# A hybrid mLSTM and differential-attention block: gate chain two pairs later, one branch gate ahead of the first q and k, merged mLSTM loads

## The chip, the cores and the metric

The kernel runs on one core of one Trainium2 chip, in one launch. The metric is the device time of that launch in microseconds (us). A core has five engines that run beside each other, each with its own instruction queue taken strictly in order: PE (TensorE, matrix products and transposes), DVE (VectorE), ACT (ScalarE), POOL (GpSimd) and SP (SyncE, which issues most of the DMAs). An instruction that has to wait holds up everything behind it on its own engine.

## The reference, cut to what matters

One layer on x of 1 x 1024 x 1024 in fp32. A normalised input is projected onto twelve segments; an mLSTM with four heads of 256 runs in both directions over one group of them, a differential attention with eight heads over another, and two gates mix the branches:

```python
h = rmsnorm(x, norm_g)
a_q, a_k, a_v, a_o, a_z, a_g, b_q, b_k, b_v, b_z, g_a, g_b = split(h @ w_in)
qk = silu(centred_depthwise_conv(concat(a_q, a_k), ml_conv_w))      # width 5
i, log_f = gates from a_g + ml_gate_b                               # 4 x 4 heads, both directions
y_a = mlstm(q, k, v, i, log_f) forward + reversed, normed, gated by a_o and a_z
y_b = (softmax(q1 k1) - lam * softmax(q2 k2)) v per head, rope, normed, gated by b_z
mix = sigmoid(g_a) * (y_a @ w_branch_a) + sigmoid(g_b) * (y_b @ w_branch_b)
out = rmsnorm(x + mix @ w_out, final_g)
```

(The last lines are told in short; the change touches none of them.)

## The kernel before, in words

**Arithmetic.** Every fp32 product is made of two float32r parts, a high one (H) and a low one (L), so a product is three matmuls: high by high, low by high, high by low. The splitting into H and L is done by ACT, DVE and POOL.

**Stages, in the order of PE's instructions.** (1) The opening: load x, normalise, transpose, first products. (2) Eighteen "pairs" of projections, numbered 0 to 17 from the list `self.pairs`: pairs 0 and 1 are wide v pairs (`wide_units`, L394, with the sink `v_sink`, L427), the others alternate a k or q pair with an o and z pair (`pair_units`, L349; sinks `conv_sink` and `oz_sink`). Each pair's products go to PSUM banks tagged T, six of them, and a sink (adds, convolution, gating on DVE, ACT and POOL) must empty a bank before PE writes it again. The products of pair i are woven with the last products of pair i - 1; a stretch of this loop is called slot i here. The sinks store the convolved q and k in DRAM tiles `cd` and v in `vd`. (3) The first head's q and k (`qk[0]`), its gate z, and the first part of v for attention (`v0`, L573). (4) Eight attention heads, each a row of eight cycles. A cycle of PE has a group of scores (S, L1062: two tiles of 128 x 1024 in PSUM, which DVE reduces, L1065, and ACT exponentiates, L1067, before PE may write them again), transposes (T) of earlier probabilities e, of att and of rb_y (L132), and the products with v. Between these, `w.weave` spreads filler: projections for the next heads and, in the last head, branch gates. (5) The mLSTM (`ml_units`), which loads k, q, v and the gates' rows back from DRAM (`load_k` L1179, `load_parts` L1185, `load_gb` L1190, `load_v` L1198, all on SP) and has nine branch gates as filler. (6) The two branch products, the mix and the output.

**Branch gates.** `gate_units` makes one gate: 48 matmuls of 128x512 in two halves. Each half ends with a tanh on ACT (`gt`, L959, one buffer) and a store into DRAM (`tgb` or `tga`, L960). During the opening and the mLSTM the store is issued by ACT, elsewhere by SP. `fill(n)` takes the next n gates of the list `gq`; `FILL[h]` says how many go into head h.

**mLSTM gates.** `ml_gates` gives pieces: the loading of the gates' weights and their products (`gl`, `gmm`), `rows` (a row computation of logs, exponentials and scans on DVE and ACT, L842 to L879, in tiles `gch`), `chain`, `weights` and `columns`. `angle_loads` gives pieces of the rotary tables (angles, then sine and cosine, which the first q and k are multiplied by at L984 to L995). The dictionary `more` puts each piece ahead of a given unit of a given pair.

**What sets the order.** PE runs in the order in which the units are added (`keep(E.PE)`). The order on DVE, ACT, POOL and SP is made by a scheduler at build time, which may move an instruction far from its place in the code; at run time each engine follows that order.

Of the kernel before, what the change touches and what calls it, by code (L numbers as in the profile page):

```python
# [36 lines left out]
INF = 1.0e9  # L37
FILL = (0, 0, 0, 0, 0, 0, 0, 2)
Z_EARLY = (0, 1, 3, 5)
# [71 lines left out]
class Block:  # L111
# [353 lines left out]
    def conv_sink(self, seg, n):  # L465
# [3 lines left out]
        def sink(i, j, ps, rest):  # L469
# [16 lines left out]
            for half in range(2):  # L486
                o = half * 512


                at = lambda x: self.cd[x][2 * n + i][:, o:o + 512]  # L490
                acc = self.psA.tile([128, 512], F32, name="pj", tag="pj", bufs=2)
                th = self.s0.tile([128, 512], F32, name="tz", tag="tz", bufs=2)
                a.mul(acc, raw[:, o:o + 512], w(0))  # L493
                for x in range(1, 5):
                    v.scalar_tensor_tensor(out=acc, in0=raw[:, o + x:o + x + 512], scalar=w(x), in1=acc, op0=ALU.mult, op1=ALU.add)  # L495
                a.activation(out=th, in_=acc, func=AF.Tanh, scale=0.5)
                yh, H = y[:, o:o + 512], raw[:, o:o + 512]
                v.scalar_tensor_tensor(out=yh, in0=th, scalar=1.0, in1=acc, op0=ALU.add, op1=ALU.mult)
                if seg == "ak":
                    self.q.dma_start(out=at("ak"), in_=yh)  # L500
                a.copy(H.bitcast(F32R), yh)
                self.q.dma_start(out=at(seg + "H"), in_=H)
                lo = th if seg == "ak" else yh
                p.tensor_tensor(out=lo.bitcast(F32R), in0=yh, in1=H, op=ALU.subtract)
                self.q.dma_start(out=at(seg + "L"), in_=lo)
        return sink
# [446 lines left out]
    def gate_units(self, seg, i):  # L953
        key = ("w_in", OFF[seg] + 128 * i)
        idx = (0 if seg == "ga" else 8) + i

        def done(half, ps):
            t = self.wpool.tile([128, 512], F32, name="gt", tag="gt")
            self.a.activation(out=t, in_=ps, func=AF.Tanh, scale=0.5, bias=self.gbh[:, idx:idx + 1])  # L959
            (self.a if self.opening or self.ml else self.q).dma_start(out=self.tg[seg][i][:, half * 512:(half + 1) * 512], in_=t)  # L960
        return sum((self.proj(key, half, lambda ps, half=half: done(half, ps)) for half in range(2)), [])
# [205 lines left out]
    def ml_head(self, n, st):  # L1167
# [8 lines left out]
        def load_k(c):  # L1176
            x = loc["ak", c] = w2.tile([128, 2, L], F32, name="akf", tag=f"kf{c}", bufs=1)
            for i in range(2):
                q.dma_start(out=x[:, i], in_=self.cd["ak"][2 * n + i][:, c * L:(c + 1) * L])  # L1179

        def load_parts(seg, c):
            st[seg, c] = tuple(w2.tile([128, 2, L], F32R, name=seg + y, tag=f"{seg}{y}{c}", bufs=1) for y in "HL")
            for x, y in zip(st[seg, c], "HL"):
                for i in range(2):
                    q.dma_start(out=x[:, i].bitcast(F32), in_=self.cd[seg + y][2 * n + i][:, c * L:(c + 1) * L])  # L1185

        def load_gb(c):
            for d in range(2):
                t = loc["gb", d, c] = w2.tile([128, L], F32, name="gb", tag=f"gb{d}{c}", bufs=1)
                q.dma_start(out=t, in_=self.gg[d, row(c):row(c) + 1, :].broadcast_to([128, L]))  # L1190

# [64 lines left out]
        def scores(tt):  # L1256
# [11 lines left out]
            for d in range(2):  # L1268
# [3 lines left out]

                p.affine_select(out=W[:, lo:hi], in_=loc["gb", d, c][:, lo:hi], pattern=[[-sg, hi - lo]], compare_op=ALU.is_ge,  # L1273
                                fill=-1.0e30, base=sg * (b * 128 - lo), channel_multiplier=sg)
# [101 lines left out]
    def ml_units(self, heads, gates):  # L1376
# [6 lines left out]
        hl = lambda x, c: x["gb"](c) + x["HL"](c)  # L1383
        for c in (3, 2, 1):
            un += x["k"](c) + x["v"](c)
        un += take(8) + x["weigh"](3, 1) + take(3) + x["state"](3, 1) + hl(x, 0)
        un += x["weigh"](2, 1) + take(5) + x["state"](2, 1) + x["k"](0) + x["v"](0)
        un += x["weigh"](1, 1) + take(4) + x["state"](1, 1) + x["split"](0) + hl(x, 1)
        un += take(4) + x["S"](0)
# [176 lines left out]
    def build(self):  # L1566
# [21 lines left out]
        with pool(name="const", bufs=1) as self.const, \  # L1588
# [18 lines left out]
            self.ya, self.yb, self.gd_ml = dt("ya"), dt("yb"), dt("gm")  # L1607
            self.cd = {n: dt("c" + n) for n in ("ak", "akH", "akL", "aqH", "aqL")}
            self.vd = {x: [[self.dram.tile([128, 512], F32, name=f"av{x}{n}_{c}") for c in range(NC)] for n in range(NH_A)] for x in "HL"}
# [60 lines left out]
            ang = [do(lambda: next(gen)) for _ in range(19)]  # L1670
            more = {(1, 0): gl + gmm}
            for (i, k), step, un in (((2, 6), 1, rows[:6]), ((4, 6), 2, rows[6:]), ((6, 6), 2, chain), ((6, 13), 1, ang[:1]),
# [3 lines left out]
                for j, u in enumerate(un):  # L1676
                    more.setdefault((i + (k + step * j) // 14, (k + step * j) % 14), []).append(u)

# [10 lines left out]
            qk, z = zip(*[self.da_proj(h, sts[h]) for h in range(NH_B)])  # L1689
            w.add(do(lambda: setattr(self, "ahead", True)), *qk[0], *z[0])  # L1690
            v0 = self.da_v(0, sts[0:2])
            w.add(*v0[:20])
            prev = None
# [92 lines left out]
```

## Time and profile before

| | before |
|---|---|
| median of 3 runs | 1704.09 us (1699.93 to 1706.28) |
| the profiled execution | 1703.18 us |
| its span in the profile | 1701.1 us |
| mean granted TensorE clock | 0.993 |
| busy: PE / DVE / ACT / POOL | 97% / 60% / 46% / 39% |
| DMA engines over the span | 117 GB/s; 191.05 MB of 199.76 MB on the queue of SP and ACT |

The span is the time from the first to the last instruction on the profile's record; the execution's own time has 2.1 us more around it. An instruction row has its start (us), its duration (us), engine, line, operation and tiles, and in brackets how long its engine had been idle and what ended the wait. Matmuls are pipelined: a matmul's own duration is longer than the distance from its start to the next one's, and it is the distance that counts for time.

### The profile page before, as it was taken

Reading aid. Unit: us, or ns where it says so; the run is one execution under the profiler, and the core shown is the slowest. Engines: PE = TensorE matmul, PEld = TensorE weight load, DVE = VectorE, ACT = ScalarE, POOL = GpSimd, SP = SyncE. Lnnn points to the kernel's source line nnn. Section 1 sums busy time; section 2 is a strip of 40 time slices with the busy share of each in tenths; the row PEclk is TensorE's granted clock in tenths of the full one; section 3 lists DMA queues with packets and bytes.
Section 4 is the critical chain, followed back from the end, with each engine's and each line's share of the span. In section 5 each row is a group of like instructions: output and inputs, shape, how many; then the busy total and the mean of one; then the engine's idle time right before and its main releaser. Section 6 shows DMA issues by size and latency. Waiting matters only on the chain. (4 is left out here: it accounts for less than half of the span.)

```text
span 1701.1 us, 25404 instructions
## 1 busy us (share of the span) xinstructions
PE 1644.1 (97%) x9335; PEld 1379.2 (81%) x9335; DVE 1025.1 (60%) x1817; ACT 775.9 (46%) x1548; POOL 660.0 (39%) x713
## 2 busy tenths in 40 slices
PE   7989999999999999999999999999999998999998
PEld 5879877778888788878878887888888876888887
DVE  5654677776754776777677677604566664235533
ACT  6433455555533455455554545524566554122221
POOL 5744666666653451524345152132132221222000
PEclk9999999999999999999999999999999999999999
DMA  5433344343342223213131221238866527453222
GB/s 183 133 109 119 125 145 149 116 137 118 130 142 69 73 54 86 69 35 85 38 100 40 73 70 44 62 102 255 257 212 204 156 75 269 145 172 101 75 91 83
DMA packets 191246, 199.76 MB, mean 117 GB/s; under 512 B 13465, under 2 KB 144882, under 8 KB 191122
## 3 DMA queue, kind: packets, MB, share of 16 engines
q1 hardware_dynamic: 187186, 191.05, 37.2%
q10 hardware_dynamic: 3936, 7.09, 1.1%
q8 instruction: 73, 1.20, 0.3%
q14 instruction: 51, 0.42, 0.1%
HBM read 124.60 MB, written 56.72 MB: 107 GB/s over the span
## 5 line engine op out<-in xcount | busy, mean ns | idle before, releaser
L551 PE MATMUL pj<-hH,wH 128*128 128x512 f32 x640 | 268.4, 419 | 1.9 <-ACT f L664 1.5
L551 PE MATMUL pj<-hH,wL 128*128 128x512 f32 x640 | 252.4, 394 | 1.6 <-POOL wL L210 1.6
L551 PE MATMUL pj<-hL,wH 128*128 128x512 f32 x640 | 251.3, 393 | 0.2 <-DVE hL L702 0.2
L1067 ACT ACTIVATE e<-S,nm 128x1024 f32<-128x1024 f32 x128 | 142.5, 1114 | 96.6 <-DVE nm L1065 96.3
L212 POOL TENSOR_TENSOR wL<-raw,wH 128x1024 fp32r<-128x1024 f32 x34 | 83.7, 2462 | 216.6 <-ACT wH L207 212.9
L1065 DVE TENSOR_REDUCE nm<-S 128x1 f32<-128x1024 f32 x128 | 150.6, 1218 | 21.7 <-PE S L1062 21.1
L551 PEld LDWEIGHTS pj<-hH,wH 128*128 128x128 f32 x640 | 121.4, 190 | 33.4 <-issue 13.1
L551 PEld LDWEIGHTS pj<-hH,wL 128*128 128x128 f32 x640 | 120.6, 188 | 31.0 <-POOL wL L210 3.6
L551 PEld LDWEIGHTS pj<-hL,wH 128*128 128x128 f32 x640 | 121.4, 190 | 17.6 <-DVE hL L702 0.6
L1087 DVE TENSOR_TENSOR pL<-T,pH 128x512 fp32r<-128x512 f32 x128 | 87.1, 687 | 65.8 <-ACT pH L1086 64.5
L551 PE MATMUL pj<-sl_yb,wH 128*128 128x512 f32 x384 | 120.3, 394 | 3.4 <-DVE sl_yb L1452 2.9
L1086 ACT CAST pH<-T 128x512 fp32r<-128x512 f32 x128 | 75.1, 587 | 80.8 <-PE T L132 79.5
L1062 PE MATMUL S<-kst,qq 64*128 64x512 f32 x768 | 106.3, 408 | 0.0
L207 ACT CAST wH<-raw 128x1024 fp32r<-128x1024 f32 x48 | 50.4, 1049 | 112.2 <-PE pj L551 88.4
L1073 DVE SCALAR_TENSOR_TENSOR e<-e,r,e 128x1024 f32<-128x1024 f32 x64 | 92.2, 1441 | 2.2
L349 PE MATMUL T<-TH,wH 128*128 128x512 f32 x256 | 87.1, 399 | 2.0 <-ACT u L356 2.0
L551 PEld LDWEIGHTS pj<-sl_yb,wH 128*128 128x128 f32 x384 | 72.8, 190 | 20.1 <-DVE sl_yb L1452 3.5
L1062 PEld LDWEIGHTS S<-kst,qq 64*128 64x128 f32 x768 | 67.8, 184 | 25.0 <-issue 11.8
L495 DVE SCALAR_TENSOR_TENSOR pj<-cin,cols,pj 128x512 f32<-128x512 f32 x128 | 86.9, 746 | 1.0 <-ACT pj L493 1.0
L349 PE MATMUL T<-TH,wL 128*128 128x512 f32 x256 | 85.9, 396 | 0.0
L132 PE MATMUL T<-ident,e 128*128 128x128 f32 x512 | 76.8, 273 | 6.4 <-ACT att L1100 4.2
L1273 POOL TENSOR_SCALAR_AFFINE_SELECT W<-gb 128x128 f32<-128x128 f32 (+1 forms) x64 | 22.7, 357 | 144.4 <-DVE W L1322 94.1
(398 smaller groups left out, 4462.8 us busy)
## 6 DMA issues: line engine op xcount, KB each, us to landing
raw<-in_w_in_dram SPq DMA_DIRECT2D x84, 512.0 KB, 4.4
kst<-hl SPq DMA_DIRECT2D x64, 128.0 KB, 2.4
qq<-hl SPq DMA_DIRECT2D x64, 128.0 KB, 2.4
x<-in_x_dram SPq DMA_DIRECT2D x8, 512.0 KB, 7.3
avH<-tz SPq DMA_DIRECT2D x16, 256.0 KB, 2.0
cak<-y SPq DMA_DIRECT2D x16, 256.0 KB, 3.4
cakH<-cin SPq DMA_DIRECT2D x16, 256.0 KB, 4.4
cakL<-tz SPq DMA_DIRECT2D x16, 256.0 KB, 3.7
```

The source lines that it names most:

```text
L132: self.t.transpose(out, in_, self.ident[0:k, 0:k])
L207: self.a.copy(wH, raw)
L212: self.p.tensor_tensor(out=wL, in0=raw, in1=wHf, op=ALU.subtract)
L349: self.t.matmul(ps, lhsT=l[:, k, :], rhs=r[:, k, :], start=(first and k == 0 and m == 0), stop=(k == 3 and m == 2), skip_group_check=not f ...
L495: v.scalar_tensor_tensor(out=acc, in0=raw[:, o + x:o + x + 512], scalar=w(x), in1=acc, op0=ALU.mult, op1=ALU.add)
L551: self.t.matmul(ps, lhsT=l[:, k, :], rhs=r, start=(n == 0), stop=(n == 23))
L1062: self.t.matmul(ps[:, o], lhsT=qq[r, x, c], rhs=k[r, y, o], start=(m == 0), stop=(m == 2))
L1065: v.tensor_reduce(out=nm, in_=ps, axis=AX.X, op=ALU.max, negate=True)
L1067: a.activation(out=e, in_=ps, func=AF.Exp, bias=nm[:, 0:1], accum_out=Z[:, j, t:t + 1])
L1073: v.scalar_tensor_tensor(out=e0, in0=e, scalar=r[:, 0:1], in1=e0, op0=ALU.mult, op1=ALU.add)
L1086: a.copy(pH[:, :, s], ps)
L1087: v.tensor_tensor(out=pL[:, :, s], in0=ps, in1=pH[:, :, s].bitcast(F32), op=ALU.subtract)
```

## The change

Four things, by part of the program.

1. **Gates' chain and angles.** Everything in `more` goes two pairs later: the gates' products from ahead of pair 1's slot to ahead of pair 3's, the rows, chain, weights and columns and all angle pieces two slots later too, so that the last angle piece stands in slot 17.
2. **A gate ahead of the first q and k.** `FILL` for head 7 goes from 2 to 1, and `fill(1)` stands ahead of `qk[0]`.
3. **Layout and loads.** The DRAM tiles `cd` get the layout [128, chunk, half, 256], so that one DMA of 256 KB loads both halves of a head's chunk, 2 KB in a row for each partition, where two DMAs of 128 KB with 1 KB in a row did. The stores keep their number and write two pieces of 1 KB for each partition, not one of 2 KB. The two DMAs that spread a gate row over the partitions (`gb`) become one. SP's instructions go from 620 rows to 557.
4. **The mLSTM's start and its gate stores.** The first head's gate rows for chunk 0 are loaded second and its q and k parts (`HL(0)`) ahead of v(1); chunk 0's k and v come a step earlier, chunk 1's rows and parts a step later. In the mLSTM the gate stores (`tgb`, `tga`) are issued by SP, not by ACT.

```diff
-FILL = (0, 0, 0, 0, 0, 0, 0, 2)
+FILL = (0, 0, 0, 0, 0, 0, 0, 1)
...
-                at = lambda x: self.cd[x][2 * n + i][:, o:o + 512]
+                ch = lambda t: t.rearrange("p (c e) -> p c e", c=2)
+                at = lambda x: self.cd[x][n][:, 2 * half:2 * half + 2, i, :]
...
                 if seg == "ak":
-                    self.q.dma_start(out=at("ak"), in_=yh)
+                    self.q.dma_start(out=at("ak"), in_=ch(yh))
                 a.copy(H.bitcast(F32R), yh)
-                self.q.dma_start(out=at(seg + "H"), in_=H)
+                self.q.dma_start(out=at(seg + "H"), in_=ch(H))
                 lo = th if seg == "ak" else yh
                 p.tensor_tensor(out=lo.bitcast(F32R), in0=yh, in1=H, op=ALU.subtract)
-                self.q.dma_start(out=at(seg + "L"), in_=lo)
+                self.q.dma_start(out=at(seg + "L"), in_=ch(lo))
...
-            (self.a if self.opening or self.ml else self.q).dma_start(out=self.tg[seg][i][:, half * 512:(half + 1) * 512], in_=t)
+            (self.a if self.opening else self.q).dma_start(out=self.tg[seg][i][:, half * 512:(half + 1) * 512], in_=t)
...
         def load_k(c):
             x = loc["ak", c] = w2.tile([128, 2, L], F32, name="akf", tag=f"kf{c}", bufs=1)
-            for i in range(2):
-                q.dma_start(out=x[:, i], in_=self.cd["ak"][2 * n + i][:, c * L:(c + 1) * L])
+            q.dma_start(out=x, in_=self.cd["ak"][n][:, c])
 
         def load_parts(seg, c):
             st[seg, c] = tuple(w2.tile([128, 2, L], F32R, name=seg + y, tag=f"{seg}{y}{c}", bufs=1) for y in "HL")
             for x, y in zip(st[seg, c], "HL"):
-                for i in range(2):
-                    q.dma_start(out=x[:, i].bitcast(F32), in_=self.cd[seg + y][2 * n + i][:, c * L:(c + 1) * L])
+                q.dma_start(out=x.bitcast(F32), in_=self.cd[seg + y][n][:, c])
 
         def load_gb(c):
-            for d in range(2):
-                t = loc["gb", d, c] = w2.tile([128, L], F32, name="gb", tag=f"gb{d}{c}", bufs=1)
-                q.dma_start(out=t, in_=self.gg[d, row(c):row(c) + 1, :].broadcast_to([128, L]))
+            t = loc["gb", c] = w2.tile([128, 2, L], F32, name="gb", tag=f"gb{c}", bufs=1)
+            q.dma_start(out=t, in_=self.gg[:, row(c):row(c) + 1, :].rearrange("d o l -> o d l").broadcast_to([128, 2, L]))
...
-                p.affine_select(out=W[:, lo:hi], in_=loc["gb", d, c][:, lo:hi], pattern=[[-sg, hi - lo]], compare_op=ALU.is_ge,
+                p.affine_select(out=W[:, lo:hi], in_=loc["gb", c][:, d, lo:hi], pattern=[[-sg, hi - lo]], compare_op=ALU.is_ge,
...
-        for c in (3, 2, 1):
-            un += x["k"](c) + x["v"](c)
-        un += take(8) + x["weigh"](3, 1) + take(3) + x["state"](3, 1) + hl(x, 0)
-        un += x["weigh"](2, 1) + take(5) + x["state"](2, 1) + x["k"](0) + x["v"](0)
-        un += x["weigh"](1, 1) + take(4) + x["state"](1, 1) + x["split"](0) + hl(x, 1)
+        un += x["k"](3) + x["gb"](0) + x["v"](3) + x["k"](2) + x["v"](2) + x["k"](1) + x["HL"](0) + x["v"](1)
+        un += take(8) + x["weigh"](3, 1) + take(3) + x["state"](3, 1) + x["k"](0) + x["v"](0)
+        un += x["weigh"](2, 1) + take(5) + x["state"](2, 1) + hl(x, 1)
+        un += x["weigh"](1, 1) + take(4) + x["state"](1, 1) + x["split"](0)
...
-            self.cd = {n: dt("c" + n) for n in ("ak", "akH", "akL", "aqH", "aqL")}
+            self.cd = {x: [self.dram.tile([128, NC, 2, L], F32, name=f"c{x}{n}") for n in range(NH_A)] for x in ("ak", "akH", "akL", "aqH", "aqL")}
...
-            more = {(1, 0): gl + gmm}
+            more = {(3, 0): gl + gmm}
...
-                    more.setdefault((i + (k + step * j) // 14, (k + step * j) % 14), []).append(u)
+                    more.setdefault((i + 2 + (k + step * j) // 14, (k + step * j) % 14), []).append(u)
...
-            w.add(do(lambda: setattr(self, "ahead", True)), *qk[0], *z[0])
             v0 = self.da_v(0, sts[0:2])
-            w.add(*v0[:20])
+            w.add(do(lambda: setattr(self, "ahead", True)), *fill(1), *qk[0], *z[0], *v0[:20])
```

The orders that come out of it, at three places. Line numbers of the changed kernel are one higher from L490 to L1178 and two lower behind its load functions.

Ahead of the first head the rows on which the first v products hang are the same in both orders: on DVE `vL` (L1042), `hl` (L994), `hl` (L995), on PE the same neighbours.

**Place 1, DVE in the pairs.** Before, the rows' computation (tiles `gch`) stands in the wide v pairs; `tz<-T,tz` at L427 is v's sink, which frees a T bank:

```order
L842 TENSOR_SCALAR gch<-gch 64x256
L843 TENSOR_TENSOR gch<-gch 64x256
L427 TENSOR_TENSOR tz<-T,tz 128x512
L846 TENSOR_SCALAR gch<-gch 64x256
L848 TENSOR_SCALAR gch<-gch 64x256
L849 TENSOR_TENSOR gch<-gch 64x256
L852 TENSOR_TENSOR gch<-gch 64x256
L853 TENSOR_TENSOR gch<-gch 64x256
L855 SCALAR_TENSOR_TENSOR gch<-gch 64x256
L861 SCALAR_TENSOR_TENSOR gch<-gch 32x256
L427 TENSOR_TENSOR tz<-T,tz 128x512
L861 SCALAR_TENSOR_TENSOR gch<-gch 32x256
```

Now, in slot 4, it stands between the gating of an o and z pair (L450) and the convolution's input of the next pair (`cin<-T`, L477):

```order
L450 SCALAR_TENSOR_TENSOR oz<-oz,T 128x512
L450 SCALAR_TENSOR_TENSOR oz<-T,oz 128x512
L853 TENSOR_TENSOR gch<-gch 64x256
L854 TENSOR_TENSOR gch<-gch 64x256
L856 SCALAR_TENSOR_TENSOR gch<-gch 64x256
L862 SCALAR_TENSOR_TENSOR gch<-gch 32x256 x2
L879 COPY gch<-gch 32x1
L892 MEMSET gch 1x64
L864 TENSOR_TENSOR gch<-gch 64x256
L477 TENSOR_TENSOR cin<-T,p_2070 128x512
L869 SCALAR_TENSOR_TENSOR gch<-gch 32x256 x2
L880 COPY gch<-gch 32x1
```

The rows' computation no longer stands between two of v's sinks; it now stands ahead of two copies of a conv sink.

**Place 2, PE in the last head,** between the fifth and the sixth group of scores (`S`); `pj` are matmuls of a branch gate. Before, the first rows of this stretch are these; a second such run of twelve `pj` follows behind the transposes of `e`, ahead of the next group of scores:

```order
L1062 MATMUL S<-kst,qq 128x512 x12
L551 MATMUL pj<-hH_207,wH 128x512
L551 MATMUL pj<-hL_209,wH 128x512
L551 MATMUL pj<-hH_207,wL 128x512
L132 MATMUL T<-ident,att 128x128 x2
L551 MATMUL pj<-hH_207,wH 128x512
L551 MATMUL pj<-hL_209,wH 128x512
L551 MATMUL pj<-hH_207,wL 128x512
L132 MATMUL T<-ident,rb_y 128x128 x4
L551 MATMUL pj<-hH_207,wH 128x512
L551 MATMUL pj<-hL_209,wH 128x512
L551 MATMUL pj<-hH_207,wL 128x512
```

Now the whole stretch is:

```order
L1063 MATMUL S<-kst,qq 128x512 x12
L132 MATMUL T<-ident,att 128x128 x2
L132 MATMUL T<-ident,rb_y 128x128 x4
L132 MATMUL T<-ident,e_10681 128x128 x8
L1063 MATMUL S<-kst,qq 128x512 x12
L552 MATMUL pj<-hH_186,wH 128x512
L552 MATMUL pj<-hL_188,wH 128x512
L552 MATMUL pj<-hH_186,wL 128x512
```

All 30 matmuls of the gate that stood between these two groups of scores are gone from there.

**Place 3, SP and ACT at the start of the mLSTM.** SP before: the rows `gb` come last but for the q and k parts:

```order
L1179 DMA akf<-cak_106 128x256
L1179 DMA akf<-cak_107 128x256
L1198 DMA vH<-avH_1_147 128x2x256
L1198 DMA vL<-avL_1_163 128x2x256
L1190 DMA gb<-gg 128x256 x2
L1185 DMA akH<-cakH_114 128x256
L1185 DMA akH<-cakH_115 128x256
L1185 DMA akL<-cakL_122 128x256
```

SP now, from k(3) on (`akf` is k, `avH_3` v of chunk 3, `tgb` a gate store):

```order
L1179 DMA akf<-cak_106 128x512
L961 DMA tgb_78<-gt 128x512
L1188 DMA gb<-gg 128x2x256
L1196 DMA vH<-avH_3_129 128x2x256
L1196 DMA vL<-avL_3_145 128x2x256
L1179 DMA akf<-cak_106 128x512
L1196 DMA vH<-avH_2_128 128x2x256
L1196 DMA vL<-avL_2_144 128x2x256
L1179 DMA akf<-cak_106 128x512
L1184 DMA akH<-cakH_110 128x512
L1184 DMA akL<-cakL_114 128x512
L1184 DMA aqH<-caqH_118 128x512
```

`gb` is second, the parts of q and k stand ahead of v(1), and the gate stores stand among the loads. ACT a few chunks on, before; `tgb_80<-gt` is a gate store, `W` and `hm` belong to the mLSTM's chunk:

```order
L207 CAST wH<-raw 128x1024
L1218 ACTIVATE kwH<-T,gc_ws 128x256
L959 ACTIVATE gt<-pj,gbh 128x512
L1252 CAST CH_11764<-C_11473 128x516
L960 DMA tgb_80<-gt 128x512
L1316 ACTIVATE hm<-I,al 128x256
L1320 ACTIVATE W_11646<-W_11646,rr 128x256
L1347 ACTIVATE PO,ssq<-hm 128x256
```

ACT there now:

```order
L207 CAST wH<-raw 128x1024
L1216 ACTIVATE kwH<-T,gc_ws 128x256
L960 ACTIVATE gt<-pj,gbh 128x512
L1250 CAST CH_11722<-C_11452 128x516
L1318 ACTIVATE W_11610<-W_11610,rr 128x256
L1314 ACTIVATE hm<-I,al 128x256
L1345 ACTIVATE PO,ssq<-hm 128x256
```

The gate's store is gone from ACT's queue; on SP it now stands ahead of loads.

## The prediction

> **What bounds the kernel now.** I read the shares and slices of the page first, then what PE waited for, then PE's starts in the places where it stood still. The chain of waits that ended last covers 1% of the span and says nothing here.
>
> ```profile
> span 1701.1 us, 25404 instructions
> PE 1644.1 (97%) x9335; PEld 1379.2 (81%) x9335; DVE 1025.1 (60%) x1817; ACT 775.9 (46%) x1548; POOL 660.0 (39%) x713
> ...
> PE T L394 <- DVE tz L427: 7.5, 1, 7.5
> PE T L132 <- ACT W L1320: 4.8, 6, 1.6
> ...
> PE T L128 <- POOL wL L210: 2.1, 1, 2.1
> ```
>
> PE is busy for 97% of the span. The change leaves PE's matmuls the same in number and form, so it can only move PE's waits (engine and tile that waited, the one it waited for, us in total, times, longest) and the clock behind them. The clock is in the windows (busy us of each engine and the mean granted clock, PEclk):
>
> ```profile
> 125.00:150.00 25.00, 21.62 (x167) 21.63 (x168) 13.33 (x20) 5.45 (x8) 7.93 (x5) 0.86 0.24 80
> 181.00:201.00 20.00, 20.00 (x88) 16.24 (x87) 14.20 (x20) 10.72 (x19) 10.57 (x9) 1.00 0.30 95
> 201.00:220.60 19.60, 19.34 (x84) 15.39 (x83) 11.99 (x17) 9.28 (x18) 15.39 (x16) 1.00 0.61 199
> 500.00:525.00 25.00, 22.84 (x145) 21.20 (x144) 4.90 (x9) 3.46 (x7) 17.24 (x15) 0.93 0.41 101
> 1150.00:1175.00 25.00, 22.74 (x119) 19.13 (x118) 7.70 (x25) 8.72 (x17) 4.93 (x13) 0.93 0.87 248
> 1200.00:1225.00 25.00, 23.37 (x154) 21.12 (x153) 14.28 (x53) 12.84 (x32) 6.40 (x18) 0.93 0.91 275
> 1150.00:1235.00 85.00, 80.13 (x487) 70.21 (x486) 44.07 (x160) 41.91 (x99) 20.74 (x54) 0.96 0.87 254
> ```
>
> Four of these places fall below 1.00: 0.86 in the first row is 0.14 x 25 = 3.5 us of missing cycles, 0.93 in three others 1.75 us each. They are the places of PE's larger gaps.
>
> **The chain two pairs later.** What made the longest wait stands on DVE:
>
> ```profile
> 116.58 2.04 DVE L846 TENSOR_SCALAR gch<-gch 64x256 f32<-64x256 f32 x1
> ...
> 124.58 2.44 DVE L855 SCALAR_TENSOR_TENSOR gch<-gch 64x256 f32<-64x256 f32 x1
> ...
> 127.67 0.65 DVE L427 TENSOR_TENSOR tz<-T,tz 128x512 fp32r<-128x512 f32 x1
> ...
> 112.90:131.60 18.70, 0.00 (x0) 0.00 (x0) 14.09 (x18) 1.25 (x3) 0.00 (x0) 0.83 0.38 115
> ...
> 119.78 0.28 PE L394 MATMUL T<-wH,TL 128*128 128x256 f32 x1
> 119.90 0.28 PE L394 MATMUL T<-wL,TH 128*128 128x256 f32 x1
> ...
> 128.38 0.58 PE L394 MATMUL T<-wH,TH 128*128 128x256 f32 x1 [7.50 <-DVE tz L427]
> ...
> 129.18 0.41 PE L394 MATMUL T<-wH,TH 128*128 128x256 f32 x1
> 129.39 0.41 PE L394 MATMUL T<-wH,TL 128*128 128x256 f32 x1
> ```
>
> The `tz` of v's sink (127.67) frees PE's T bank. In DVE's order it stands behind the rows' computation, of which the first and the last of four slow instructions are shown (2.04 and 2.44 us for 256 elements, where the sink takes 0.65 for 512); in all `gch` holds DVE for 14.09 us. PE starts at 128.38 after 7.50 us, and then its matmuls are 0.22 us apart, not 0.12 (119.78, 119.90): half clock. Half clock for 7 us makes the 3.5 us of missing cycles; I put 3.0 us of it inside the gap, where it costs nothing, which leaves about 4 us at half clock, or 1.9 us lost. This place costs 7.5 + 1.9 = 9.4 us. With the rows' computation out of the wide pairs no such block stands ahead of `tz`: **-9.4**.
>
> What is late next? The 14 us now fall on DVE in slots 3 and 4. By the windows DVE is busy 14.20 of 20 us and 11.99 of 19.6 there, so 13.4 us are free: just about what is needed, and less if the slow instructions come back. The new order puts part of the block ahead of two `cin<-T` copies (L477). But those free banks that PE wants only in a later slot, where `tz` was wanted at once: of six T banks a pair here takes three, so a sink has about one slot (20 us) of slack. I take **+1** for small waits; the bounds are 0 and 14.1, the whole block in PE's way.
>
> Angles and tables too end two slots later; the gate ahead of the first q and k (48 matmuls at 0.23 us, 11 us) covers that. Without it the sine and cosine would stand about 10 us ahead of their use and could be late, a stall like the 2 to 4 us at L573 below. Its matmuls are neither gained nor lost, only moved.
>
> **The place before the heads.** Does that gate also remove the wait at L573?
>
> ```profile
> 514.73 0.43 DVE L1042 TENSOR_TENSOR vL<-pj,vH 128x256 fp32r<-128x256 f32 x1 [6.97 <-ACT vH L1041]
> ...
> 515.71 0.68 DVE L995 TENSOR_TENSOR hl<-pj,cosT 128x512 f32<-128x512 f32 x1
> ...
> 516.44 0.39 PE L573 MATMUL pj<-wH,hH 128*128 128x256 f32 x1 [2.16 <-DVE hl L995]
> ```
>
> DVE takes `vL` first, which waits for ACT's part of the first v product; only then `hl` at L994 and L995, which free the bank for the second. The new order has the same sequence on DVE and the same neighbours on PE. The 2.2 us and the 1.75 us of clock stay: **0**; if they went, -3.9.
>
> **The last head.** It loses the gate's 11 us of filler, and between its fifth and sixth group of scores none is left. The stretch before:
>
> ```profile
> 1069.04 1.66 PE L1062 MATMUL S<-kst,qq 64*128 64x512 f32 x12
> ...
> 1070.64 0.51 PE L551 MATMUL pj<-hH,wH 128*128 128x512 f32 x1
> ...
> 1077.16 0.39 PE L551 MATMUL pj<-hH,wL 128*128 128x512 f32 x1
> 1077.39 0.40 PE L551 MATMUL pj<-hH,wH 128*128 128x512 f32 x1
> ...
> 1079.31 0.51 PE L1062 MATMUL S<-kst,qq 64*128 64x512 f32 x2
> ...
> 1088.64 1.65 PE L1062 MATMUL S<-kst,qq 64*128 64x512 f32 x12
> ...
> 1096.39 0.50 PE L1062 MATMUL S<-kst,qq 64*128 64x512 f32 x2
> ...
> 1070.74 2.36 DVE L1065 TENSOR_REDUCE nm<-S 128x1 f32<-128x1024 f32 x2 [0.23 <-PE S L1062]
> ...
> 1073.49 1.11 ACT L1067 ACTIVATE e<-S,nm 128x1024 f32<-128x1024 f32 x1
> ```
>
> From the first scores to the next it is 1079.31 - 1069.04 = 10.3 us; the 30 matmuls that fall out stand 0.23 us apart (1077.16, 1077.39), 6.9 us, so 3.4 us of PE's work remain, 1.6 of them the scores (to 1070.64). But the next scores go into the same PSUM tiles: DVE's two reductions end at 1073.10 and ACT's second exponential, the last to read them, at 1073.49 + 1.11 = 1074.60, 5.56 us after the scores began. So PE waits 5.56 - 3.4 = 2.2 us. Behind the seventh group (1088.64 to 1096.39) 12 matmuls fall out: 7.75 - 2.76 = 5.0 us remain, a wait of 0.6. With something for the other cycles, which lose three matmuls each: **+3**; bounds 1.5 (the exponential's start is held a little by small instructions of ACT that may go elsewhere) and 5 (one half-clock stretch of 1.75 on top).
>
> **The mLSTM.** Two kinds of waits, both by way of ACT's queue:
>
> ```profile
> 1155.85 0.65 POOL L1273 TENSOR_SCALAR_AFFINE_SELECT W<-gb 128x128 f32<-128x128 f32 x2 [10.02 <-DMA gb<-gg]
> ...
> 1160.53 0.58 ACT L1215 COPY kn<-T 128x512 f32<-128x512 f32 x1 [0.41 <-ACT gt L959]
> ...
> 1161.59 0.36 PE L128 MATMUL T<-vH,kwH 128*128 128x258 f32 x1 [2.13 <-POOL wL L210]
> ...
> 1208.33 0.63 ACT L1252 CAST CH<-C 128x516 fp32r<-128x516 f32 x1
> 1212.22 0.33 ACTq L960 DMA_DIRECT2D tgb<-gt  x1
> ...
> 1213.56 0.71 PE L132 MATMUL T<-ident,W 128*128 128x128 f32 x2 [1.57 <-ACT W L1320]
> ```
>
> First, POOL's masks wait 10 us for `gb`, ACT's W and everything behind it (`wH`, `gt`, `kn`) run late, and `kn` only at 1160.53, and PE stands 2.13 us (the wait bears the name of POOL's wL, but PE's next product needs what ACT and DVE make from `kn`). With `gb` loaded second this goes: 2.1 + 1.75 (window 1150 to 1175) = 3.9 us. Second, a gate store on ACT (1212.22) stands in line for a DMA slot from 1208.96 to 1212.22; W at L1320 comes late and PE waits 1.57 us. The row of waits on W L1320 has 4.8 us in 6 such waits, all in the mLSTM; with 1.75 of clock (window 1200 to 1225) 6.5 us. Together at most 10.4 us.
>
> In exchange SP carries the stores in line with the loads: a store that waits for ACT's `gt` holds the loads behind it. And the loads are no smaller: the DMA engines are 0.87 busy at 254 GB/s between 1150 and 1235 us, and v(1) now stands behind 1 MB of q and k parts (1 MB at 254 GB/s is 4 us). Half as many DMAs save SP's issue time, no bytes. I take two thirds: **-7**; bounds -10.4 and 0 (every wait of ACT turned into one for a load).
>
> The Trainium skill, "DMA: Bandwidth & Descriptors", section "Issuing engines are not separate DMA queues", speaks against the second part: issuing from another engine saves only the sequencer's issue time. By it six stores at some 0.33 us would be worth 2 us and the sum 4 us higher. The trace disagrees for this kernel: ACT stood 3.3 us in line before it issued one store, with work behind it.
>
> **The sum.** 1703.2 (the profiled execution) - 9.4 + 1 + 0 + 3 - 7 = **1691 us**. That execution is 0.9 us under the median of 1704.09, which I leave inside the range.
>
> **The rivals.**
> 1. *The loads hold the mLSTM.* The DMA engines are 87% busy there, and SP waits for ACT in front of loads; the waits turn into waits for v(1) or k(0). Against it: the waits of before end on ACT's queue, not on a load that PE needs. The mLSTM's term is 0: 1698 us.
> 2. *The wait before the heads goes after all.* The gate gives DVE and ACT 11 us there. Against it: the order quoted. 1691 - 3.9 = 1687 us.
> 3. *The half clock stays in the mLSTM.* Two gaps of 2.13 and 1.57 us, at 1161.59 and 1213.56, are followed by it. If it comes from the many short matmuls around them rather than from the gaps, 3.5 us stay: 1694.5 us. The Trainium skill, "TensorE: Matmul & The Clock Gate", section "Why this matters for your kernels", has the clock fall only behind gaps of more than about 3 us. By that rule these gaps would not have done it; the rows show 0.93 around each of them, so I hold to the rows.
> 4. *Slower: the block starves the pairs.* The 14.09 us of DVE work do not fit into 13.4 us of free time if the copies' bank is wanted at once, and PE waits for a `cin<-T`. It decides when a sink's slack is below the block's length. Then +14.1 in place of +1; with the last head at its bound (+5) and no gain in the mLSTM the sum is 1703.2 - 9.4 + 14.1 + 5 = 1713 us. With only half the block in the way it is near 1706.
> 5. *The change does not do what it says* is out: the orders show the block moved, the filler gone and ACT's stores gone.
>
> **How the numbers follow.** The forecast has 0.50, rival 1 0.20, rival 2 0.10, rival 3 0.10, rival 4 0.10. A measurement of this kernel tells 0.5% (8.5 us) from no change, so faster means below 1695.6 and slower above 1712.6. The forecast's own spread (bounds of the last head, the pairs and the mLSTM) puts nine tenths of it below 1695.6, 0.45; rival 2 adds 0.10, rival 3 0.07 and the lower edge of rival 1 0.02: faster 0.64. Slower is half of rival 4, 0.05. The rest, 0.31, is within. The range goes from 1682 (the forecast with all 10.4 us of the mLSTM, no new wait in the pairs and rival 2: 1703.2 - 9.4 + 3 - 10.4 - 3.9 = 1682.5) to 1702, which takes in rival 1 with 4 us more and leaves out rival 4.
>
> **What would show it.** Right: no wait for `tz` at L427 and a clock of 1.00 in the pairs; the wait at L573 of about 2.2 us still there; a wait of PE for ACT's e (L1067) of about 2.2 us in the last head; ACT's rows free of DMA issues in the mLSTM and the wait for W L1320 well under 4.8 us. Wrong: a wait of several us for `cin` or an oz row in slots 3 to 6; PE waiting for `vH`, `akf` or `aqL` from DMA in the mLSTM; or a clock of 0.93 at places that had none.

## The result, and the profile after

| | before | after |
|---|---|---|
| median | 1703.44 us (1699.93 to 1706.28, 4 runs) | 1691.48 us (1689.61 to 1693.39, 4 runs) |
| ratio | | 0.9931, 95% interval 0.9908 to 0.9954 |
| the profiled execution / its span | 1703.18 / 1701.1 us | 1692.50 / 1690.7 us |

The changed kernel is 12 us faster. The time on record, 1691, was met; the terms of its sum were not all. Two executions far outside all others (2002.84 us at a granted clock of 0.753 for the combined kernel below, 3254.38 us for the kernel before) are left out of every median and ratio. First the head of the changed kernel's page, where PE is as full as before:

```profile
span 1690.7 us, 25288 instructions
PE 1640.5 (97%) x9335; PEld 1377.7 (81%) x9335; DVE 1019.6 (60%) x1817; ACT 774.9 (46%) x1548; POOL 660.4 (39%) x713
```

Then what its PE waited for (us in total, times, longest):

```profile
PE T L349 <- ACT u L356: 3.7, 4, 1.5
PE T L128 <- ACT kwH L1216: 3.0, 4, 2.4
PE pj L574 <- DVE hl L996: 2.2, 1, 2.2
PE pj L552 <- DVE sl_yb L1449: 2.1, 1, 2.1
PE T L132 <- ACT W L1318: 1.9, 3, 0.7
...
PE T L132 <- DVE zg L1131: 1.2, 1, 1.2
```

The 7.5 us for v's `tz` are gone, and so is the 2.1 us wait by the name of wL L210 in the mLSTM; the waits on W fell from 4.8 to 1.9 us, the wait for `hl` is unchanged. New are 2.4 of the 3.0 us on `kwH` (one wait), 1.2 us on `zg` in the last head, and 1.7 us more on `u` in the pairs. The windows of the same places, with the granted clock behind the busy times:

```profile
125.00:150.00 25.00, 25.00 (x192) 23.96 (x191) 10.49 (x13) 10.58 (x19) 12.61 (x10) 1.00 0.35 130
181.00:201.00 20.00, 20.00 (x88) 16.15 (x87) 19.24 (x28) 11.50 (x22) 14.28 (x15) 1.00 0.55 172
201.00:220.60 19.60, 19.60 (x87) 15.86 (x86) 18.76 (x27) 12.13 (x21) 13.05 (x10) 1.00 0.37 103
510.00:535.00 25.00, 22.85 (x164) 21.51 (x164) 3.77 (x7) 2.63 (x6) 10.12 (x9) 0.93 0.40 95
1125.00:1150.00 25.00, 22.60 (x107) 18.46 (x105) 1.98 (x3) 7.21 (x16) 10.46 (x31) 0.98 0.51 156
1150.00:1175.00 25.00, 25.00 (x130) 21.74 (x130) 8.69 (x28) 8.64 (x17) 4.09 (x10) 0.89 0.85 272
1200.00:1225.00 25.00, 25.00 (x174) 22.99 (x173) 16.58 (x61) 15.97 (x39) 6.89 (x18) 1.00 0.78 246
```

The wide v pairs run at full clock without a gap. In slots 3 and 4 DVE is now busy 19.24 of 20.0 us and 18.76 of 19.6, where before it was 14.20 and 11.99, and PE is full beside it. In place of the mLSTM's two half clocks of before (1.75 us of missing cycles each) one of twice the length stands at its start (0.02 x 25 + 0.11 x 25 = 3.25 us).

Where the time went is best read from when each stage begins on PE. The lengths of the stages in us, from the profiles of both and of the experiments below (a gate of 10.9 us stands in another stage where it was moved):

| stage | before | after | chain alone | stores alone | no gate ahead | two gates ahead | old load order |
|---|---|---|---|---|---|---|---|
| start to the pairs' last matmul | 486.4 | 479.7 | 479.5 | 487.4 | 478.7 | 479.9 | 479.4 |
| to the first scores | 41.8 | 52.7 | 40.3 | 40.3 | 40.3 | 63.6 | 52.7 |
| heads 0 to 6 | 506.8 | 506.9 | 507.0 | 506.9 | 507.9 | 506.1 | 506.0 |
| last head, to the mLSTM's first state | 114.3 | 110.0 | 114.3 | 114.3 | 117.2 | 111.4 | 107.4 |
| mLSTM, to its last product | 249.4 | 240.2 | 249.3 | 238.9 | 239.5 | 238.7 | 239.0 |
| the rest | 302.4 | 301.2 | 303.9 | 301.5 | 300.9 | 302.0 | 302.4 |

From before to after: the pairs -6.7, the last head -4.3 with 10.9 us of work less in it, the mLSTM -9.2, the rest -1.2. The wait on `kwH` at the mLSTM's first state counts to the last head's stage: 2.4 us after, 2.7 with no gate and with two gates ahead, none in the others.

### The profile page after: what moved, and what is told of

Read it like the earlier page. It is cut to its first block, busy times and chain, and to the rows that moved or that the text cites. A ratio compares the mean times of both kernels' runs of the same rounds, so it can differ in the third digit from the quotient of the medians.

```text
span 1690.7 us, 25288 instructions
## 1 busy us (share of the span) xinstructions
PE 1640.5 (97%) x9335; PEld 1377.7 (81%) x9335; DVE 1019.6 (60%) x1817; ACT 774.9 (46%) x1548; POOL 660.4 (39%) x713
## 5 line engine op out<-in xcount | busy, mean ns | idle before, releaser
L574 PE MATMUL pj<-wH,hH 128*128 128x256 f32 x256 | 76.1, 297 | 2.2 <-DVE hl L996 2.2
```

The costliest lines, as they stand in the source:

```text
L574: self.t.matmul(ps[:, i, :], lhsT=l, rhs=r[:, k, :], start=(kh == 0 and k == 0 and m == 0), stop=(kh == 1 and k == 3 and m == 2))
```

## The experiments

Each edit is against the changed kernel unless it says before. Times are medians, ratios against the kernel before measured beside it.

**No gate ahead.** What does the moved gate buy?

```diff
-FILL = (0, 0, 0, 0, 0, 0, 0, 1)
+FILL = (0, 0, 0, 0, 0, 0, 0, 2)
...
-            w.add(..., *fill(1), *qk[0], *z[0], *v0[:20])
+            w.add(..., *qk[0], *z[0], *v0[:20])
```

> The changed kernel, but with both gates in the last head again and none ahead of the first q and k. Theory: the gate ahead covers nothing. In the changed kernel the last table piece (L794) ends at 475.2 us and the pairs' last matmul starts at 479.7, so the first use of the tables, 5.5 us of products later, would not wait. The last head gets its filler back (the time from its first scores to the mLSTM's first state, 105.7 us less gate, loses some 4 us). Time 1691 - 4 = 1687 us; first scores 10.9 us earlier than in the changed kernel (521.5). Rival, the prediction's: the gate is a cover, and a wait of 2 to 4 us appears at the first q and k; time 1690 to 1692 us, first scores at 523.5 to 525.5.

1683.97 us (1682.78 to 1686.3), ratio 0.9883 (0.9867 to 0.9899). The first scores come at 519.0 us; no wait appears at the first q and k. PE's waits in the last head of the changed kernel:

```profile
PE T L132 <- DVE zg L1131: 1.2, 1, 1.2
PE T L132 <- ACT att L1101: 1.1, 2, 0.6
PE T L132 <- DVE pL L1088: 0.8, 1, 0.8
PE T L132 <- ACT T L1111: 0.4, 1, 0.4
PE S L1063 <- ACT e L1068: 0.4, 1, 0.4
```

With both gates in the last head only this one is left:

```profile
PE T L132 <- ACT att L1101: 1.2, 2, 0.6
```

The row on `att`, 1.2 us, stands in the kernel before as well; the rest, 2.8 us, is the filler's absence. The stage with the last head takes 117.2 us with both gates and 110.0 with one; of the 10.9 us of a gate only 7.2 are saved there and 3.7 are lost, 0.9 more than the rows show. The gate ahead of the first q and k covered nothing. The time moved by 7.5 us, where 4 were expected, so both kernels were run again side by side.

> The changed kernel with both gates in the last head again, for its distance to the changed kernel on one chip: theory 4 us by the waits that the profile shows in the last head (1687.5), rival 7.5 us as the first runs had it, the rest being half clocks that follow the waits by chance (1684).

> The changed kernel itself again, as the measure for the three others of this call: 1691.5 us, within 2 us.

No gate ahead 1686.02 us (1681.46 to 1690.28, ratio 0.9900, 0.9881 to 0.9919), changed kernel 1692.87 (1689.91 to 1694.91, ratio 0.9941, 0.9925 to 0.9957): 6.9 us. The mean granted clock of the six runs each was 0.9958 and 0.9943. The difference, 0.0015 of 1690 us, is 2.5 us of cycles: with the 3.7 to 4.1 us lost in the last head (110.3 and 117.1 us for the stage in these two profiles) that is 6.2 to 6.6 of the 6.9 us, so the theory of 4 us was too low and the rival nearer. The table shows where 1.5 of the 2.5 us go: to the first scores it takes 40.3 us with no gate ahead, 52.7 with one and 63.6 with two, 1.5 more than the gates' own 10.9 and 21.8. That is the half clock behind the wait for `hl`, which stands in all six profiles with a gate ahead of the first q and k and in one of the five others that have this wait. Where the rest goes, the profiles do not tell.

**Two gates ahead.** The suspected cost doubled: `FILL` 0 for the last head, `fill(2)` ahead.

> The changed kernel with the suspected cost doubled: both gates ahead of the first q and k, none in the last head. Theory: the last head's groups of scores cannot follow each other in less than some 5.5 us (reductions and exponentials of the PSUM tiles); three of its cycles now have 2.7 to 3.4 us of PE work, where the changed kernel has one with 3.1 and one with 4.7; so 2.2 to 2.9 us are lost in each, some 7.4 us in place of 3.7: 1695 us, with half clocks up to 1698. Rival: the cost of the gate ahead lies elsewhere (at the start or by chance), and the time stays at 1691.5 us.

1702.47 us (1699.61 to 1705.25, 10 runs), ratio 0.9997 (0.9986 to 1.0008): 9.6 us above the changed kernel measured beside it. The direction was right, the price too small: 1698 us was the highest forecast. PE's waits in the last head:

```profile
PE S L1063 <- ACT e L1068: 3.3, 4, 1.3
PE T L132 <- DVE pL L1088: 1.7, 3, 0.8
PE T L132 <- DVE zg L1131: 1.2, 1, 1.2
PE T L1099 <- DVE pL L1088: 1.2, 1, 1.2
```

And two windows of it:

```profile
1066.00:1091.00 25.00, 21.62 (x124) 16.41 (x125) 21.46 (x31) 14.94 (x32) 4.09 (x8) 0.86 0.03 11
1091.00:1116.00 25.00, 21.07 (x119) 16.99 (x119) 13.45 (x18) 11.49 (x27) 4.06 (x4) 0.86 0.11 32
```

Now the scores wait for the exponentials (`e`), as the prediction had it, four times, and the transposes behind them wait too; and PE runs at 0.86 in both windows, 7 us of missing cycles in 50 us. The cost is not in proportion to the filler that is taken: with both gates in the last head nothing is lost beyond the row on `att`, with one 3.7 us, with none 16 (111.4 against 117.2 with 21.8 us of work less), the 7 us of missing cycles among them; the theory had 7.4.

**The gate between q, k and v.** `*qk[0], *z[0], *fill(1), *v0[:20]`: can the wait at L574 be had out?

> The changed kernel, but the gate that stands ahead of the first q and k stands between them and the first v of the attention. On DVE hl (L995, L996) then stands ahead of vL. Theory: the wait at L574 (2.15 us, with a half clock of 3.4 us behind it, 1.7 us lost) is DVE's order alone and goes: 3.9 us less, 1687.5 us, no half clock near 515 us. Rival: hl of the second half waits for the transfers out of the first (one buffer, landed at 514.3 in the changed kernel), and a part of 1 to 2 us stays. Second rival: q and k without the gate ahead wait for their tables: a new wait of 2 to 4 us near 485 us.

1690.46 us (1687.89 to 1691.53), ratio 0.9917 (0.9900 to 0.9933). PE's waits from 480 to 600 us:

```profile
PE T L132 <- ACT att L1101: 1.1, 1, 1.1
PE S L1063 <- ACT e L1068: 1.0, 1, 1.0
PE pj L552 <- ACT gt L960: 0.8, 1, 0.8
PE T L1099 <- DVE pL L1088: 0.8, 1, 0.8
```

The wait for `hl` is gone, so it was the order on DVE, and q and k did not wait for tables. From the pairs' end to the first scores it is 48.5 us, 4.2 less than after. But heads 0 to 6 take 509.1 us, 2.2 more, with the new waits for `e` and `pL` in the first head, and the time is within the spread of the changed kernel: the 1687.5 us of the theory were not met.

**Gate stores alone.** The kernel before, with only this:

```diff
-            (self.a if self.opening or self.ml else self.q).dma_start(out=self.tg...
+            (self.a if self.opening else self.q).dma_start(out=self.tg...
```

> The kernel before with one part of the change alone: in the mLSTM SP issues the gate stores. Theory: ACT no longer stands in line, PE's waits on W L1320 fall from 4.8 us to under 2.5, the half clock near 1214 us goes, and the time falls by 4 to 7 us: 1697 to 1699 us. Rival: the gain needs the merged loads as well, since with twice the number of loads SP is the one that stands in line and the loads behind a store come late: within 2 us of the kernel before, 1702 to 1705 us.

1693.16 us (1691.18 to 1695.91), ratio 0.9934 (0.9915 to 0.9954): more than the theory had. PE's waits in the mLSTM:

```profile
PE T L132 <- ACT W L1320: 1.9, 3, 0.7
...
PE T L128 <- POOL wL L210: 0.4, 1, 0.4
```

And ACT's rows at the place where in the kernel before `kn` came only at 1160.53:

```profile
1155.49 0.87 ACT L1275 ACTIVATE W<-W,gc_negM 128x128 f32<-128x128 f32 x2 [2.46 <-POOL W L1273]
1156.26 1.04 ACT L207 CAST wH<-raw 128x1024 fp32r<-128x1024 f32 x1
1157.20 0.68 ACT L959 ACTIVATE gt<-pj,gbh 128x512 f32<-128x512 f32 x1
1157.78 0.80 ACT L1275 ACTIVATE W<-W,gc_negM 128x256 f32<-128x256 f32 x2
1158.49 0.57 ACT L1215 COPY kn<-T 128x512 f32<-128x512 f32 x1
```

The waits on W went from 4.8 to 1.9 us, exactly as far as in the changed kernel, and no half clock is left in the mLSTM. And the wait by the name of wL L210 went from 2.1 to 0.4, though `gb` is loaded as late as before: without the store in its queue ACT has a new order, in which `wH` and `gt` run between the two pairs of W while the second `gb` is awaited, and `kn` starts 2 us earlier.

**Gate stores on ACT again,** the same line undone in the changed kernel.

> The changed kernel, but ACT issues the gate stores in the mLSTM again. Theory: the stores wait in ACT's queue for a DMA slot, W at L1318 comes late again, and the stretch from the first state to the last I product is 4 to 6 us longer: time 1695 to 1697 us, waits of PE on W L1318 near the 4.8 us of before (1.9 in the changed kernel). Rival: only the issue time counts, some 0.33 us for each of six stores with work behind it: 2 us longer, 1693 us. Second rival: the merged loads already took the cause away (half as many DMAs in the line), and nothing changes: 1691 us.

1699.01 us (1696.01 to 1701.1, 9 runs), ratio 0.9972 (0.9961 to 0.9983). The profiled execution was the fastest of the nine; its waits on W are only 2.4 us and its mLSTM 1.4 us longer than after. So the runs give a price of 7.5 us, more than the 4 to 6 of the theory, without the sign that it named, waits on W near 4.8. Nor is it time in line (from the end of ACT's instruction before a store to the store's issue): in the kernel before, ACT stands 8.8 us in all in front of four of its stores (2.0, 3.3, 1.3 and 2.3), here 1.3 us in front of one. Where the slower executions lose the 7.5 us is open.

What a store in line waits for shows in the kernel before, at the store of 1212.22:

```profile
1212.60 0.39 ACT L1347 ACTIVATE PO<-hm 128x256 f32<-128x256 f32 x1 [3.63 <-DMA gb<-gg]
```

The store needs nothing of `gb`. But in the traces the DMAs of SP and ACT take eight semaphores in turn, and this store has that of a `gb` load that SP issued eight DMAs earlier, at 1206.21, and whose last landing is at 1212.14.

**The old load order** (the four lines of `ml_units` as before, loads merged).

> The changed kernel, but with the old order of the first head's loads in the mLSTM (gb behind v(1), parts of chunk 0 behind it). Theory from the two profiles: the early gb moved a wait, it did not remove it (before 2.13 us at the second state and a half clock of 3.4 us; now 2.40 us at the first state and a half clock of 6.8 us). So the old order puts the wait back to the second state and the time is the same or up to 2 us lower: 1689 to 1691.5 us. Rival, the prediction's: early rows are worth 3.9 us; 1695 us.

1689.65 us (1688.08 to 1690.73), ratio 0.9915 (0.9897 to 0.9934). The early `gb` brought nothing; whether it costs 2 us is not told apart from none. What the changed kernel made of it, on SP, POOL, ACT and PE:

```profile
1140.79 0.43 SPq L1188 DMA_DIRECT2D gb<-gg  x1
...
1147.05 1.24 POOL L1271 TENSOR_SCALAR_AFFINE_SELECT W<-gb 128x128 f32<-128x128 f32 x4 [3.76 <-DMA gb<-gg]
...
1147.37 0.86 ACT L1273 ACTIVATE W<-W,gc_negM 128x128 f32<-128x128 f32 x2 [6.98 <-POOL W L1271]
1148.14 0.67 ACT L960 ACTIVATE gt<-pj,gbh 128x512 f32<-128x512 f32 x1
1148.71 0.46 ACT L1216 ACTIVATE kwH<-T,gc_ws 128x256 fp32r<-128x256 f32 x1
...
1149.27 0.55 PE L128 MATMUL T<-vH,kwH 128*128 128x258 f32 x1 [2.40 <-ACT kwH L1216]
```

`gb` is issued at 1140.79 and POOL starts on it at 1147.05: it lands 6 us later, among the large loads. But ACT's order, made at build time, now has the first W ahead of the first state's `kwH`. So ACT waits 7 us for POOL, `kwH` runs at 1148.71, and PE stands 2.40 us at the first state. The wait was moved by one state, not removed. With the old order nothing waits there (the last head's stage is 107.4 us, not 110.0), and no half clock stands in the mLSTM.

**Split loads.** Each merged load as two again, in the new layout:

```diff
-            q.dma_start(out=x, in_=self.cd["ak"][n][:, c])
+            for i in range(2):
+                q.dma_start(out=x[:, i], in_=self.cd["ak"][n][:, c, i])
...
```

> The changed kernel, but each merged load of 256 KB split into two of 128 KB again, with 1 KB in a row for each partition, and gb into two; order, stores and layout as changed. Theory: the bytes are the same and the DMA engines are the limit there (0.85 to 0.96 busy between 1150 and 1200 us in the changed kernel), so the merge itself is worth little: 1691 to 1693 us. Rival: twice the number of transfers in the line holds SP (each waits for the one eight before it), the gate stores and the loads behind them come later, and the mLSTM's stretch gets 3 to 5 us longer: 1695 us.

1692.02 us (1689.83 to 1693.62), ratio 0.9926 (0.9908 to 0.9943): the merge itself is not measurable. The 2.4 us wait on `kwH` is not there, and one wait for a load appears, which the changed kernel does not have:

```profile
PE T L128 <- DMA vH<-avH: 1.6, 1, 1.6
```

The window with the busiest DMA engines (the last two columns are their share and GB/s), with split loads:

```profile
1150.00:1235.00 85.00, 83.33 (x532) 74.18 (x532) 48.13 (x176) 46.54 (x109) 20.21 (x53) 1.00 0.85 251
```

The same window of the changed kernel:

```profile
1150.00:1235.00 85.00, 84.18 (x525) 75.07 (x525) 47.81 (x175) 45.68 (x107) 19.83 (x51) 0.97 0.84 266
```

0.85 busy at 251 GB/s, against 0.84 at 266.

**Chain alone.** The kernel before with the two lines on `more`.

> The kernel before with one part of the change alone: everything in the dictionary of gate and angle pieces two pairs later; both gates in the last head, loads and gate stores as before. Theory: the pairs give what they gave in the changed kernel, where their last matmul came 6.7 us earlier than before; the tables are not late (the kernel without the gate ahead showed no wait there), and nothing behind the pairs changes: 1703.4 - 6.7 = 1696.7 us. Rival: without the gate ahead the first q and k wait for their tables (2 to 4 us): 1699 to 1701 us. Second rival: the pairs' gain is lost to half clocks or waits later, 1700 us or more.

1692.44 us (1689.52 to 1696.48), ratio 0.9931 (0.9909 to 0.9953), 4 us less than the theory had. The pairs give 6.9 us in its profile; the rest of the distance to before is not in any stage of that one execution (1696.48, the slowest of the four, against 1703.18). Its waits on W L1320 are 6.4 us, so the mLSTM's part is still to be had.

**Three edits combined:** both gates in the last head, the old load order, and two buffers for `hl` (`tag="hl", bufs=2`), so that DVE takes `hl` ahead of `vL`.

> The changed kernel with three edits at once: both gates in the last head and none ahead of the first q and k, the old order of the first mLSTM loads, and two buffers for hl, so that DVE takes hl (L995, L996) ahead of vL and the wait at L574 goes. Theory: the edits add: 1684.0 (no gate ahead) - 1.8 (old load order) - 2.2 (wait at L574, no half clock behind it in the kernel without the gate ahead) = 1680 us. Rival: the first head, which begins 2.2 us earlier, loses this again to its own waits, as with the gate between (there 2.2 of 4.2 us were lost in the first head): 1682 us. Second rival: two buffers cost elsewhere, 1684 us or more.

1682.37 us (1680.47 to 1686.28), ratio 0.9878 (0.9856 to 0.9899), 2.4 us above the theory.

> The combined kernel again (both gates in the last head, old order of the first mLSTM loads, two buffers for hl). Theory: its profile had neither the wait at L574 nor waits of the last head, so it lies under the kernel that only has both gates in the last head by the 2 to 4 us of those two edits: 1680 to 1682.5 us. Rival: the first four runs' distance (1682.4 against 1684.0) is noise, and both come out equal.

1683.88 us (1683.65 to 1684.77, 3 runs), ratio 0.9887 (0.9867 to 0.9907), above the 1680 to 1682.5 of the theory. The wait for `hl` is gone in both profiles. From the pairs' end to the first scores it takes 37.9 us in both profiles, 2.4 less than with one buffer and no gate ahead. Against no gate ahead (1684.0 and 1686.0) it is 1.6 and 2.1 us lower, within the intervals: the best kernel of the study, 18 to 21 us or 1.1 to 1.2% under before, but its two smaller edits are not shown one by one.

## Why the prediction was right, and where it was not

**The total** was met (1691 against 1691.48) because errors cancelled, which is luck. By the runs of single parts, the chain alone takes 10.8 us (8.4 were written) and the stores alone 10.0 (7 for the whole mLSTM), and the gate ahead costs 6.9 to 7.5 (3 were written for the last head); the early `gb` costs 0 to 2 and the merged loads nothing that is measurable. These add to 11.3 to 13.9 us, and 12 were measured.

**The chain: the mechanism was right.** -9.4 + 1 = -8.4 was written. The wait for `tz` and its half clock are gone; new waits in the pairs took back 2.7 us (1.7 more on `u` L356, 1.0 on `pj` and `oz`) where +1 was written, so the stage is 6.7 us shorter. The chain alone gives 11 us by runs, with an interval of 8 to 15; the 8.4 lies at its edge, the 6.7 below it. Rival 4, that the block starves the pairs, is out: DVE is full in slots 3 and 4 and PE does not wait there. That a sink of these pairs has about a slot of slack was an argument; the windows agree with it. Why the block was slow, the prediction does not ask. In the kernel before each of its four slow instructions (2.0 to 2.4 us, where others of 64x256 take 0.4) runs beside an instruction of POOL of 2.4 us and ends at most 0.3 us after it: at 118.62, 121.10, 124.54 and 127.02 us, POOL's at 118.47, 120.95, 124.26 and 126.75. That POOL holds them is read from these times; no run here tries it.

**The cover: wrong, and without a price.** "The gate ahead of the first q and k covers that" had no wait to cover: without it the time is 7 us less.

**The place before the heads: right.** The `hl` wait stayed at 2.15 us, so rival 2 is out, and with the gate between it went, so DVE's order was the cause. That its half clock always follows was wrong, as the last section shows.

**The last head: a loss, as forecast, but by other waits and somewhat larger.** +3 was written, and a wait of 2.2 us for `e` was named as the sign. From the first of the two scores to the next it took 5.34 us (1071.94 to 1077.28) where 5.56 was forecast, but the waits came ahead of the scores, at the transposes, and the only wait for `e` in this head is 0.4 us:

```profile
1071.94 1.65 PE L1063 MATMUL S<-kst,qq 64*128 64x512 f32 x12
...
1074.82 0.66 PE L132 MATMUL T<-ident,e 128*128 128x128 f32 x4 [0.42 <-ACT T L1111]
1076.70 0.66 PE L132 MATMUL T<-ident,e 128*128 128x128 f32 x4 [1.22 <-DVE zg L1131]
1077.28 2.10 PE L1063 MATMUL S<-kst,qq 64*128 64x512 f32 x12
```

They wait for the banks that ACT's and DVE's work on `att` and `rb_y` holds, and DVE does that work behind its reductions. That the time between the scores came out so near is in part luck: with all filler gone the exponentials do limit it (3.3 us on `e` with two gates ahead), with one gate it is the transposes' banks. In all the last head lost 3.7 to 4.1 us in the profiles. The term was 0.7 to 1.1 us too small. Against the kernel with no gate ahead the runs give 6.9 to 7.5 us for the gate's place; 1.5 of these are the half clock behind `hl`, which the kernel before has as well, and the rest is not located.

**The mLSTM: the sum nearly right, one step wrong.** -7 was written; the stage gave 9.2 us, of which 2.4 went into the wait on `kwH` ahead of it. Of the 3.5 us of missing cycles that were to go, 3.25 stayed, now behind that wait. The step that failed is "With `gb` loaded second this goes: 3.9 us". The late `gb` made ACT wait, but what PE waited for was ACT's order behind it, and the order changed with each edit: the stores alone took that wait away, and the early `gb` put one of 2.4 us at another place. "I take two thirds" of the stores' gain was too cautious: SP in line with stores and loads cost nothing that the runs show. Rival 1, that the loads hold the mLSTM, appears only as 1.6 us on `vH`, and only with split loads.

The rule of the Trainium skill, "DMA: Bandwidth & Descriptors", section "Issuing engines are not separate DMA queues", gave about 2 us for the move of the stores, worked out in the prediction for six of them; the two experiments on that edit give 10 and 7.5. The edit moves 19 stores (ACT's DMA issues fall from 29 to 10), 6.2 us of issue time at 0.33 each. The 10 us are more than all of that: with the old loads ACT also stood 8.8 us in line, and its order changed. How the price divides among the three is not shown, since the 7.5 us come with only 1.3 us in line.

**Rival 3, the half clock,** is half true. In the mLSTM it goes with the gaps: with the stores alone or the old load order, where the waits of 2 us at its start are not there, it is gone. But a sign that the prediction named for being wrong, a clock of 0.93 at a place that had none, came true behind the mLSTM's last product. The changed kernel there, then the kernel before at the same work:

```profile
1395.00:1420.00 25.00, 24.24 (x104) 19.59 (x105) 10.97 (x10) 11.90 (x17) 3.48 (x4) 0.93 0.75 257
...
1400.00:1425.00 25.00, 23.76 (x109) 18.91 (x108) 10.21 (x13) 12.83 (x20) 7.39 (x10) 1.00 0.63 203
```

The longest waits of PE just before it are 0.54 and 0.50 us, on `hm`, and the kernel before has the same two. So no single long gap is needed, as the rival had it; what makes the difference is open.

## What to carry to other kernels

Where PE is busy for 97% of the span, time is won in waits of 1 to 8 us, and each has to be asked which queue it stands in: moving DMA issues off an engine with urgent work was worth 7 to 10 us here, halving the number of the loads nothing that could be measured. An order made at build time moves with every edit, so a load that comes earlier can pull its consumer ahead of something more urgent; look at the order of the engine in between, not only at the load. Filler has a place: a cycle that waits for its own chain (5.3 us here) needs it more than a place that a guess says is uncovered. One experiment that undoes this part alone shows which is which.

## What was not expected of the hardware

The same wait is followed by a half clock in one profile and not in another. In the changed kernel the `hl` wait of 2.15 us (window 510 to 535, above) has 0.93; in the kernel without the gate ahead, where it is as long, the clock stays at 1.00:

```profile
508.79 0.39 PE L574 MATMUL pj<-wH,hH 128*128 128x256 f32 x1 [2.16 <-DVE hl L996]
...
498.00:523.00 25.00, 22.84 (x176) 21.50 (x175) 5.09 (x8) 3.63 (x7) 10.32 (x9) 1.00 0.40 96
```

At this place it may belong to the kernel: six profiles of six with a gate ahead have it, one of five without. At another it changes between two profiles of one kernel. The window with the 2.13 us wait for `sl_yb` has 1.00 in the changed kernel's first profile:

```profile
1420.00:1445.00 25.00, 22.39 (x97) 17.75 (x96) 13.30 (x11) 9.41 (x10) 5.54 (x3) 1.00 0.85 301
```

In its second profile it has 0.93:

```profile
1420.00:1445.00 25.00, 22.65 (x93) 18.45 (x94) 11.99 (x9) 6.16 (x7) 7.24 (x3) 0.93 0.79 275
```

Over all profiles a half clock stands at 7 of the 11 `hl` waits and at 11 of the 14 `sl_yb` waits. A stretch at half clock is mostly 3.41 us long, some are two or three times that, and one of 3.41 misses 1.7 us of cycles. Such stretches make up most of the scatter of this kernel: the six runs with no gate ahead go from 1681.46 us at a mean clock of 0.999 to 1690.28 at 0.994, and 0.005 of 1686 us is 8.4 of these 8.8 us. The Trainium skill, "TensorE: Matmul & The Clock Gate", section "What's actually happening", has a window of 3413 ns that runs freely and does not start with the kernel; the length of the stretches agrees with it, and it would fit a place that falls now inside and now outside. The rule of the Trainium skill, "TensorE: Matmul & The Clock Gate", section "Why this matters for your kernels", to avoid gaps of more than about 3 us, does not hold as a limit here, since these gaps are 2.1 us. For a prediction such a stretch behind a gap of 2.1 us is a chance, 18 of 25 in these profiles, not a sure term.
